# Where fourteen operand slots of a diffusion backbone lie in SBUF

## Chip, cores and metric

The kernel runs on one core of a Trainium2 chip. The metric is the device time of one execution in microseconds (us), smaller is better. "Offset" below is an SBUF address within a partition, in bytes, modulo 256.

## What is computed

A two-layer diffusion backbone over 512 latent tokens (LAT) with a prefix of 256 context tokens (CTX), width 1024, in float32:

```python
def swiglu(h, w_in, w_out):
    gate, up = jnp.split(h @ w_in, 2, axis=-1)
    return (jax.nn.silu(gate) * up) @ w_out
...
# layer i: half-step SwiGLU -> mixer (0 = short gated conv, 1 = GQA) -> half-step SwiGLU
h = norm_modulate(x_lat, norm_g[i, 0], m_lat[:, 0, 0], m_lat[:, 0, 1])
x_lat = x_lat + MACARON_WEIGHT * m_lat[:, 0, 2] * swiglu(h, ffn_w_in[i, 0], ffn_w_out[i, 0])
...
return rms_norm(x_lat, final_g)
```

Every sub-layer starts with an RMS norm, scaled and shifted by vectors that come from a conditioning vector, and ends in a gated residual. Layer 0 mixes by a gated convolution of width 3, layer 1 by attention with 8 query heads, 2 key heads and a two-dimensional rotary embedding. The FFN is 2816 wide.

## The kernel before

**Arithmetic.** A float32 product is made of three fp32r matmuls (mm3, lines 860 to 863): weights high x operand high (L861), weights high x operand low (L862), weights low x operand high (L863). "High" is the rounded value, "low" the remainder; ScalarE makes the high part and VectorE the low part (split, L189 and L190). Activations lie transposed, with features on the partitions and tokens along the free dimension, so the activation is the moving operand and a 128 x 128 block of weights the stationary one. Each matmul has its own weight load, which the profile lists as PEld.

**Seven products.** The first matmul of an FFN and of the convolution is done by a fast 2 x 2 scheme over halves of the features and of the tokens: seven products M1 to M7 take the place of eight. Each output chunk c takes one round. In a round TensorE runs M1 (operand B11), M2 (B21), M7 of the chunk before (T3), M5 (T1), M6 (T2), and of the chunk before M4 (T4) and M3 (B22). A product is 4 k-steps of 3 matmuls, 12 matmuls of 384 columns, or of 256 columns in the last FFN, where only the 512 latent tokens are left. The first two or three chunks of a sub-layer are done directly, with operands B11, B21, B12 and B22, while the sums T1 to T4 are still being made. The order is written out by hand (product_order) for TensorE and SyncE, and for stretches of VectorE and ScalarE.

**Slots.** The operands' high and low parts lie in fourteen slots of the pool xp, tags T0 to T13:

- in the rounds (T_SLOTS, line 68): B11 in 0 and 1, B21 in 2 and 3, B12 and later T4 in 4 and 5, T1 in 6 and 7, B22 in 8 and 9, T2 in 10 and 11, T3 in 12 and 13; in the last FFN (LAST_T_SLOTS, line 73) B12 and T4 in 6 and 7, T1 in 8 and 13, B22 in 9 and 10, T2 in 11 and 12, T3 in 4 and 5;
- when the rounds are over, slots 6 and 7, 10 and 11, 8 and 9 hold the last weights of the closing matmul (HELD_AFTER_T, line 71; "f00held", "c01held", "f02held" and "f10held" in the profile, three output blocks in each of the first two pairs, two in the third), and other pairs in the last FFN and the attention;
- between times they hold the normed tokens before the split, the first conditioning weights, the QKV operands (h in 0 to 3, hl in 4, 5, 8 and 9), the attention's probabilities p (0 to 3), its queries and its output.

The other matmul operands are the streamed weights w (pool wp), the gated activations gh and gl (tags G0 to G3), and vh and vl of the attention; all of them lie at offset 96 before and after.

**How a slot gets its place.** The pool x_all (24576 bytes, offset 96) comes first in xp. A tag of xp gets its place when the first tile with this tag is asked for, right behind the tag before, and it is as large as its largest tile. A tile of [4, 384] float32 has 6144 bytes = 24 x 256. Slots 4, 5, 8 and 9 also hold B12 and B22 of the very first FFN, which carry two more columns: [4, 386], 6176 bytes = 6144 + 32. So each of these four slots moves the offset of everything behind it by 32. The first use is by the conditioning weights (slots 6, 7, 8, then 9, 10, 11, then 4, 5, then 13), then by B11, B21 (0 to 3) and the normed tokens (12).

Of the kernel before, what the change touches and what calls it, by code (L numbers as in the profile page):

```python
# [10 lines left out]
F32 = mybir.dt.float32  # L11
# [7 lines left out]
P = 128  # L19
D = 1024  # L20
# [47 lines left out]
T_SLOTS = {"B11": (0, 1), "B21": (2, 3), "B12": (4, 5), "T4": (4, 5), "T1": (6, 7), "B22": (8, 9), "T2": (10, 11), "T3": (12, 13)}  # L68

F_SLOTS = {(0, 0): 12, (1, 0): 13, (0, 1): 10, (1, 1): 11}  # L70
HELD_AFTER_T = ((6, 7), (10, 11), (8, 9))

LAST_T_SLOTS = {"B11": (0, 1), "B21": (2, 3), "B12": (6, 7), "T4": (6, 7), "T1": (8, 13), "B22": (9, 10), "T2": (11, 12), "T3": (4, 5)}
# [56 lines left out]
def backbone(ctx: ExitStack, tc: tile.TileContext, a: dict, out: bass.AP):  # L130
# [4 lines left out]
    xp = ctx.enter_context(tc.tile_pool(name="xp", bufs=1))  # L135
# [202 lines left out]
    def add_products(key, sources, order, parts, direct, out_w, held, home=lambda c, kh: None, between=None):  # L338

        raw = {}  # L340
        seen = set()

        def need(c, which):
            if (c, which) not in raw:
                raw[c, which] = raw_add(sources[c][which], (1, KC), 2 if c < direct else 1)

        for c, which in ((0, 0), (0, 1), (1, 0), (1, 1)):
            need(c, which)
        for c, m in order:
            if m == "out":  # L350
                last = c == len(parts) - 1
                outs = out_w(c)
                add_out(*outs, held=held if last else None, key=f"{key}held", events=((key, "M5"), (key, "M6"), (key, "M3")))
                continue
            for which in range(2):
                need(c, which)
            if (c, m) == (0, "10") and between:
                between()
            if c >= direct:
                add_product(raw[c, 0], raw[c, 1], m)  # L360
            elif (c, m[1]) not in seen:
                seen.add((c, m[1]))
                k0 = 4 * int(m[1])
                for which in range(2):
                    where = home(c, int(m[1]))
                    add_plain(raw[c, which], 0, slice(k0, k0 + 4), where and ("home", (*where, which)))
# [46 lines left out]
    def w_list():  # L413
        def ffn_products(i, s, home=lambda c, kh: None, between=None):
            b = 2 * i + s // 2
            boot = (i, s) == (0, 0)
            held = {(1, 0): HELD_AFTER_T[:2], (1, 2): HELD_AFTER_LAST_T}.get((i, s), HELD_AFTER_T)
            sources = [[a["ffn_w_in"][b, f][:, z] for z in range(2)] for f in range(FC)]
            f0 = starts(FFN_PARTS)
            add_products(f"f{i}{s}", sources, ffn_order[boot], FFN_PARTS, BOOT_DIRECT if boot else FFN_DIRECT, lambda p: (a["ffn_w_out"][b], f0[p], FFN_PARTS[p]), held, home, between)  # L420
# [7 lines left out]
        sources = [[a["conv_w_in"][j][:, u] for j, u in pair] for pair in conv_pairs]  # L428
        add_products("c01", sources, conv_order, (6, 6), CONV_DIRECT, lambda p: (a["conv_w_out"], 4 * p, 4), HELD_AFTER_T)
        ffn_products(0, 2)  # L430
# [159 lines left out]


    x_all = xp.tile([P, KC, NT], F32, name="x", tag="x")
    stage = {}
    ssq = []
    hh, hl = [None] * KC, [None] * KC
# [125 lines left out]
    T, full = {}, {}  # L721
    geo = SimpleNamespace(tokens=TOKENS, half=NH, groups=BOTH, t_slots=T_SLOTS, f_slots=F_SLOTS)
    region = []
# [1171 lines left out]
```

## Time and profile before

| | |
|---|---|
| time, median of 3 runs | 2406.66 us (2406.36 to 2406.87) |
| span of the profiled execution | 2405.2 us |
| busy: TensorE, weight loads | 2383.8 us (99%), 2258.6 us (94%) |
| busy: VectorE, ScalarE, GpSimd | 2033.0 us (85%), 1164.8 us (48%), 135.2 us (6%) |
| granted TensorE clock | 0.999 |
| read from HBM | 249.16 MB, 104 GB/s over the span |

Busy time counts an instruction from its start to its end. Matmuls overlap: the next one starts before the one ahead of it has ended, so a matmul of 384 columns is listed with some 0.34 us while the next starts some 0.17 us later. What adds up to the span is the distance from start to start. The timeline shows starts to 0.01 us, so the pace of a group is read over many matmuls: the start of one product less the start of the product before is the time of 12.

### The profile page before, as it was taken

How to read it: one execution, taken by the hardware profiler on the slowest of the kernel's cores; microseconds unless marked ns; L12 is line 12 of the kernel's file. 1: busy time of each engine (PE TensorE's matmuls, PEld its weight loads, DVE VectorE, ACT ScalarE, POOL GpSimd, SP SyncE). 2: the span in 40 equal slices, each digit the busy share in tenths (PEclk: the TensorE clock that was granted, in tenths of full speed). 3: DMA queues.
4: the chain of work that ended last, by engine and by line, in shares of the span. 5: the costliest groups of instructions: out<-in, count | busy, mean ns of one | idle time of the engine just before them, and what ended most of it. 6: DMA issues, size and time to landing. Idle time of an engine off the chain costs nothing.

```text
span 2405.2 us, 37639 instructions
## 1 busy us (share of the span) xinstructions
PE 2383.8 (99%) x14303; PEld 2258.6 (94%) x14303; DVE 2033.0 (85%) x4018; ACT 1164.8 (48%) x2198; POOL 135.2 (6%) x256
## 2 busy tenths in 40 slices
PE   8999999999999999999999999999999999999998
PEld 6999999999999999999999999999998889999998
DVE  6989989978988888888887988888778987987787
ACT  5634334355535653433435543343355776555555
POOL 0001111100000001000000001101100000000000
PEclk9999999999999999999999999999999999999999
DMA  9234444430334123323432144443441101133331
GB/s 334 87 112 137 130 126 129 131 115 27 106 106 132 33 69 115 127 93 119 126 100 73 49 124 126 146 136 122 141 131 45 53 10 58 67 110 102 106 106 62
DMA packets 93062, 253.71 MB, mean 105 GB/s; under 512 B 10320, under 2 KB 18640, under 8 KB 92880
## 3 DMA queue, kind: packets, MB, share of 16 engines
q1 hardware_dynamic: 71984, 183.65, 23.5%
q0 software_dynamic: 20352, 67.12, 9.4%
q8 instruction: 112, 1.84, 0.3%
q14 instruction: 70, 0.57, 0.1%
q10 hardware_dynamic: 544, 0.52, 0.1%
HBM read 249.16 MB, written 2.10 MB: 104 GB/s over the span
## 4 chain that ended last, share of the span: by engine, by line
PE 92%; DVE 3%; ACT 2%; DMA 1%; issue 1%; SPq 0%; DVEq 0%; ACTq 0%
PE ps_A L861 16%; PE ps_A L862 16%; PE ps_A L863 16%; PE ps_C L862 11%; PE ps_C L861 11%; PE ps_C L863 11%; PE ps_B L863 3%; PE ps_B L861 3%; PE ps_B L862 3%; PE ps_T L1542 1%; DMA ada<-in_ada_w 1%; ACT pr L1525 0%; DMA raw<-in_ffn_w_in 0%; DVE w L190 0%; PE ps_O L861 0%
## 5 line engine op out<-in xcount | busy, mean ns | idle before, releaser
L189 ACT ACTIVATE w<-raw 128x512 fp32r<-128x512 f32 (+1 forms) x862 | 522.4, 619 | 721.0 <-PE ps_A L863 229.7
L190 DVE TENSOR_TENSOR w<-raw,w 128x512 fp32r<-128x512 f32 (+1 forms) x862 | 574.3, 679 | 119.7 <-ACT w L189 105.8
L509 POOL DMA_DIRECT2D aw<-in_ada_t x240 | 129.1, 538 | 1374.8 <-DVE mods L530 973.9
L373 DVE TENSOR_TENSOR raw<-raw,raw 128x512 f32<-128x512 f32 x264 | 181.5, 689 | 9.0 <-DMA raw<-in_ffn_w_in 4.9
L862 PE MATMUL ps_C<-gl,w 128*128 128x512 f32 (+1 forms) x548 | 188.5, 344 | 0.0
L861 PE MATMUL ps_C<-gh,w 128*128 128x512 f32 (+1 forms) x548 | 188.4, 344 | 0.0
L863 PE MATMUL ps_C<-gh,w 128*128 128x512 f32 (+1 forms) x548 | 188.2, 343 | 0.0
L861 PE MATMUL ps_A<-gh,w 128*128 128x512 f32 (+1 forms) x540 | 185.8, 344 | 0.6 <-DVE x L929 0.6
L862 PE MATMUL ps_A<-gl,w 128*128 128x512 f32 (+1 forms) x540 | 185.7, 344 | 0.0
L863 PE MATMUL ps_A<-gh,w 128*128 128x512 f32 (+1 forms) x540 | 185.5, 344 | 0.0
L530 DVE CUSTOM_DVE_ANT_0 ps_S<-aw,silu_row,packed 128x512 f32<-128x512 f32 x208 | 156.9, 754 | 2.4 <-DMA aw<-in_ada_t 1.0
L530 DVE CUSTOM_DVE_ANT_0 ps_S<-aw,silu_row,mods 128x512 f32<-128x512 f32 x208 | 156.8, 754 | 1.0
L929 DVE SCALAR_TENSOR_TENSOR x<-ps_C,gat,x 128x512 f32<-128x512 f32 (+1 forms) x158 | 99.5, 631 | 43.1 <-PE ps_C L863 42.7
L861 PE MATMUL ps_A<-tB11h,w 128*128 128x384 f32 (+1 forms) x400 | 130.8, 327 | 0.2 <-ACT tB11h L785 0.2
L862 PE MATMUL ps_A<-tB11l,w 128*128 128x384 f32 (+1 forms) x400 | 130.3, 326 | 0.2 <-DVE tB11l L786 0.2
L863 PE MATMUL ps_A<-tB11h,w 128*128 128x384 f32 (+1 forms) x400 | 130.4, 326 | 0.0
L862 PE MATMUL ps_C<-tB22l,w 128*128 128x384 f32 (+2 forms) x376 | 121.8, 324 | 0.0
L863 PE MATMUL ps_C<-tB22h,w 128*128 128x384 f32 (+2 forms) x376 | 121.7, 324 | 0.0
L861 PE MATMUL ps_C<-tB22h,w 128*128 128x384 f32 (+2 forms) x376 | 121.5, 323 | 0.0
L929 DVE SCALAR_TENSOR_TENSOR x<-ps_A,gat,x 128x512 f32<-128x512 f32 (+1 forms) x162 | 101.8, 637 | 17.0 <-PE ps_A L863 16.7
L863 PEld LDWEIGHTS ps_C<-gh,w 128*128 128x128 f32 x548 | 103.9, 190 | 12.3
L861 PEld LDWEIGHTS ps_A<-gh,w 128*128 128x128 f32 x540 | 102.4, 190 | 14.0 <-issue 1.0
(486 smaller groups left out, 6946.0 us busy)
## 6 DMA issues: line engine op xcount, KB each, us to landing
raw<-in_ffn_w_in SPq DMA_DIRECT2D x170, 512.0 KB, 3.7
aw<-in_ada_t POOLq DMA_DIRECT2D x240, 256.0 KB, 3.0
raw<-in_ffn_w_out SPq DMA_DIRECT2D x80, 512.0 KB, 4.1
raw<-in_conv_w_in SPq DMA_DIRECT2D x24, 512.0 KB, 3.7
ada<-in_ada_w SPq DMA_DIRECT2D x28, 256.0 KB, 5.7
raw<-in_attn_w_qkv SPq DMA_DIRECT2D x12, 512.0 KB, 4.9
raw<-in_ada_w SPq DMA_DIRECT2D x8, 512.0 KB, 6.8
silu_row<-in_crow POOLq DMA_DIRECT2D x8, 512.0 KB, 4.2
```

What stands on the lines that cost most here:

```text
L189: hi = act.activation(dsth, src, AF.Copy)
L190: lo = dve.tensor_tensor(out=dstl, in0=src, in1=dsth.bitcast(F32), op=ALU.subtract)
L373: dve.tensor_tensor(out=quad(o), in0=quad(x), in1=quad(y), op=ALU.subtract)
L509: nc.gpsimd.dma_start(w, a["ada_t"][t, kh, j])
L530: ins = dve.tensor_tensor_reduce(out=junk, in0=w, in1=silu_row[kh][:, v, :], scale=1.0, scalar=total if kh else ada_b[:, i, hm // 2, col : ...
L861: pe.matmul(ps, wh, xh, start=first, stop=False, **kw)
L862: pe.matmul(ps, wh, xl, start=False, stop=False, **kw)
L863: pe.matmul(ps, wl, xh, start=False, stop=last, **kw)
L929: dve.scalar_tensor_tensor(out=x, in0=p[:, o - off : o - off + w], scalar=gat[:, m, v : v + 1], in1=x, op0=ALU.mult, op1=ALU.add)
L1542: pe.transpose(pt[:, c, :], pr[:, (c0 + c) * P : (c0 + c + 1) * P], ident)
```

## The change

Two additions: a list of the slots, and a loop that asks for one tile of each tag in this order right after x_all, before anything else does. These tiles are never written or read. The shape is [3, 512] float32, 6144 bytes; the four tags with a larger tile later keep their 6176 bytes.

```diff
 F_SLOTS = {(0, 0): 12, (1, 0): 13, (0, 1): 10, (1, 1): 11}
+SLOT_ORDER = (6, 7, 10, 11, 12, 0, 1, 2, 3, 13, 8, 9, 4, 5)
 HELD_AFTER_T = ((6, 7), (10, 11), (8, 9))
...
     x_all = xp.tile([P, KC, NT], F32, name="x", tag="x")
+    for n in SLOT_ORDER:
+        xp.tile([P, 3, D // 2], F32, name=f"slot{n}", tag=f"T{n}")
```

Offsets of the slots in the built programs, in the order in which they lie:

| | 96 | 128 | 160 | 192 | 224 |
|---|---|---|---|---|---|
| before | 6, 7, 8 | 9 | 10, 11, 4 | 5 | 13, 0, 1, 2, 3, 12 |
| after | 6, 7, 10, 11, 12, 0, 1, 2, 3, 13, 8 | 9 | 4 | 5 | none |

The slots take the same stretch of SBUF as before, from byte 28768 to 114912, and nothing outside it moves. On each engine the two programs have the same instructions with the same operands, waits and signals in the same order; the addresses in them are all that differs.

## Prediction

> **What bounds the kernel now.** I read the page first, for the bound, then the waits of TensorE, then the costliest groups by form, and last the timeline, row by row, where one operand changes and nothing else does.
>
> ```profile
> span 2405.2 us, 37639 instructions
> ...
> PE 2383.8 (99%) x14303; PEld 2258.6 (94%) x14303; DVE 2033.0 (85%) x4018; ACT 1164.8 (48%) x2198; POOL 135.2 (6%) x256
> ...
> PE 92%; DVE 3%; ACT 2%; DMA 1%; issue 1%; SPq 0%; DVEq 0%; ACTq 0%
> ```
>
> ```profile
> PE ps_C L484 <- DMA ada<-in_ada_w: 4.6, 2, 4.2
> ```
>
> TensorE is busy 99% of the span and 92% of the chain that ended last; its longest wait in total is 4.6 us, at the start. So the time is the sum of the gaps between starts of matmuls, and what one gap gains the span gains. VectorE, at 85%, has room for a TensorE that goes a third of a per cent faster. The instructions keep their order and their waits, so all that the change can move is the length of single operations.
>
> A round of the seven products, 12 matmuls of 384 columns each, all with weights at offset 96 (modulo 256), looks so in the timeline (columns: start in us, duration):
>
> ```profile
> 901.09 0.34 PE L861 MATMUL ps_A<-tB11h,w 128*128 128x384 f32 x1
> ...
> 903.21 0.34 PE L861 MATMUL ps_B<-tB21h,w 128*128 128x384 f32 x1
> ...
> 905.32 0.34 PE L861 MATMUL ps_A<-tT3h,w 128*128 128x384 f32 x1
> ...
> 907.42 0.34 PE L861 MATMUL ps_C<-tT1h,w 128*128 128x384 f32 x1
> ...
> 909.51 0.33 PE L861 MATMUL ps_A<-tT2h,w 128*128 128x384 f32 x1
> ...
> 911.59 0.34 PE L861 MATMUL ps_A<-tT4h,w 128*128 128x384 f32 x1
> ...
> 913.69 0.34 PE L861 MATMUL ps_C<-tB22h,w 128*128 128x384 f32 x1
> ...
> 915.77 0.40 PE L861 MATMUL ps_C<-gh,w 128*128 128x512 f32 x1
> ```
>
> The same work takes 2.12, 2.11 and 2.10 us for B11, B21 and T3 (slots at 224), 2.09 for T1 (both at 96), 2.08 for T2 (160), 2.10 for T4 (160 and 192) and 2.08 for B22 (96 and 128). That is 6.33 us / 36 = 175.8 ns a matmul at 224 against 2.09 / 12 = 174.2 for T1.
>
> Is it the offset or the product? The closing pass of an FFN holds the moving operand still (g, at 96) and changes only the slots that hold the weights, in the order (6,7), (10,11), (8,9):
>
> ```profile
> 1275.56 0.34 PE L861 MATMUL ps_C<-gh,f02held 128*128 128x384 f32 x1
> ...
> 1281.81 0.34 PE L861 MATMUL ps_C<-gh,f02held 128*128 128x384 f32 x1
> ...
> 1288.16 0.33 PE L861 MATMUL ps_A<-gh,f02held 128*128 128x384 f32 x1
> ```
>
> 36 matmuls with weights in slots 6, 7 (at 96, like g) take 6.25 us, 173.6 ns each; the next 36, with weights in 10, 11 (at 160), take 6.35 us, 176.4 each. Slots 6 to 11 are neighbours in memory, the shapes are equal and no wait lies between. What counts, then, is how the offset of one operand stands to that of the other; equal offsets are among the best. With 512 and 256 columns (layer 1):
>
> ```profile
> 1787.77 0.40 PE L861 MATMUL ps_C<-gh,f10held 128*128 128x512 f32 x1
> ...
> 1795.94 0.40 PE L861 MATMUL ps_C<-gh,f10held 128*128 128x512 f32 x1
> ...
> 1804.34 0.39 PE L861 MATMUL ps_A<-gh,w 128*128 128x512 f32 x1
> ...
> 1809.81 0.28 PE L861 MATMUL ps_C<-gh,f10held 128*128 128x256 f32 x1
> ...
> 1814.12 0.39 PE L647 MATMUL ps_S<-th,ones_r 128*128 128x512 f32 x1
> ...
> 1814.58 0.28 PE L861 MATMUL ps_A<-gh,f10held 128*128 128x256 f32 x1
> ...
> 1818.82 0.28 PE L861 MATMUL ps_C<-gh,w 128*128 128x256 f32 x1
> ```
>
> At 512 columns equal offsets take 8.17 / 36 = 226.9 ns, weights at 160 take 8.40 / 36 = 233.3. At 256 columns the sign turns: 4.31 / 36 = 119.7 with equal offsets against 4.24 / 36 = 117.8 at 160. So the change gains on long matmuls and loses on short ones.
>
> **The change part by part.** It removes, adds and moves no instruction; the two new lines only fix places. Ten slots (6, 7, 10, 11, 12, 0, 1, 2, 3, 13) come to 96, the offset of w, g, vh and vl; slots 8, 9, 4 and 5 keep 96, 128, 160 and 192. So B22, T4 and B12 keep their price. The counts:
>
> ```profile
> L861 PE MATMUL ps_A<-tB11h,w 128*128 128x384 f32 x312 | 106.0, 340 | 0.2 <-ACT tB11h L785 0.2
> ...
> L861 PE MATMUL ps_B<-tB21h,w 128*128 128x384 f32 x272 | 92.1, 339 | 0.0
> ...
> L861 PE MATMUL ps_A<-tT3h,w 128*128 128x384 f32 x272 | 92.0, 338 | 0.0
> ...
> L861 PE MATMUL ps_C<-tT1h,w 128*128 128x384 f32 x272 | 91.2, 335 | 0.0
> ...
> L861 PE MATMUL ps_C<-tB11h,w 128*128 128x384 f32 x40 | 13.5, 338 | 0.0
> ...
> L861 PE MATMUL ps_A<-tB21h,w 128*128 128x384 f32 x32 | 11.1, 347 | 0.0
> ...
> L861 PE MATMUL ps_C<-tB21h,w 128*128 128x384 f32 x32 | 10.8, 338 | 0.0
> ```
>
> 1. *Slots 0 to 3, 12 and 13 from 224 to 96, 384 columns.* 312 + 272 + 272 + 40 + 32 + 32 = 960 triples of L861 to L863, 2880 matmuls. 175.8 becomes what equal offsets show: 174.2 at worst (T1, which follows a product at 224), 173.6 at best (36 in a row). After the change five products in a row are equal, so I take 173.6: 2880 x 2.2 ns = -6.3 us (ends -4.6 and -6.3). The mean durations say the same, 338 to 340 against 335; no other group differs in so many rows.
> 2. *T1, already at 96*, loses the neighbour at 224: 816 x 0.6 = -0.5 us (0 to -0.5).
> 3. *T2 from 160 to 96* (as many as T1): 2.08 / 12 = 173.3 becomes 173.6, +0.2 us (0 to +0.7, the upper end at 174.2).
> 4. *Weights held in slots 10, 11.* Three closing passes at 384 columns use them in two halves of 36: 216 x 2.8 = -0.6 us. In layer 1, 36 x 6.4 = -0.2 us. The pair (8,9) keeps its offsets. Nothing hides this, as TensorE does not wait there.
> 5. *QKV, 512 columns*: h lies in slots 0 to 3.
>
> ```profile
> L861 PE MATMUL ps_A<-gh,w 128*128 128x512 f32 x306 | 119.5, 391 | 0.6 <-DVE x L929 0.6
> ...
> L861 PE MATMUL ps_A<-h,w 128*128 128x512 f32 x64 | 25.2, 394 | 0.0
> ...
> L861 PE MATMUL ps_B<-h,w 128*128 128x512 f32 x16 | 6.3, 394 | 0.0
> ```
>
> h takes 3 ns more than g. 3 x (64 + 16) are 240 matmuls; hl stays where it is, so I take most of the difference, 2.5 ns: -0.6 us (0 to -1.0).
>
> 6. *The last FFN and the attention, 256 columns.* Three products of a round of the last FFN, and behind them the count of a product's k-steps there (20 rounds of 4) and of the attention's matmuls on p, from the groups by form:
>
> ```profile
> 2116.31 0.28 PE L861 MATMUL ps_A<-tT2h,w 128*128 128x256 f32 x1
> ...
> 2117.72 0.28 PE L861 MATMUL ps_A<-tT4h,w 128*128 128x256 f32 x1
> ...
> 2119.14 0.28 PE L861 MATMUL ps_C<-tB22h,w 128*128 128x256 f32 x1
> ```
>
> ```profile
> L861 PE MATMUL ps_O<-p,vh 128*128 128x256 f32 x96 | 28.3, 295 | 0.0
> ...
> L861 PE MATMUL ps_A<-tT2h,w 128*128 128x256 f32 x80 | 22.4, 281 | 0.0
> ```
>
> T2 (160 and 224 in that stage) takes 1.41 us for 12, 117.5 ns each, T4 (both at 96) 1.42, 118.3. After the change B11, B21, T1 and T2 join T4: 5 x 240 matmuls at most at the 119.7 of the held weights, at least at T4's own 118.3. From some 118 that is 1200 x 1.7 = +2.0 at the top, +0.3 at the bottom. The 3 x 96 matmuls on p (slots 0 to 3, now equal to vh and vl) give 0 to 288 x 1.7 = +0.5 by the same step, and the few weights held in these stages I put at 0 to +0.2, an estimate from the same 1.7. The two ends are equally near, so I take the middle, +1.4 us (+0.3 to +2.7; middle 1.5, less a little as T4 is the nearer row).
>
> 7. *Other engines on the moved slots.*
>
> ```profile
> L802 DVE TENSOR_TENSOR tB11l<-f,tB11h 128x768 fp32r<-128x768 f32 x8 | 7.6, 951 | 1.0 <-ACT tB11h L800 1.0
> ...
> L190 DVE TENSOR_TENSOR tT1l<-f,tT1h 128x768 fp32r<-128x768 f32 x8 | 7.3, 954 | 0.1
> ```
>
> VectorE takes 951 ns at 224 and 954 at 96: nothing. What is late next is nothing either: a round that is 0.1 us shorter needs the same splits, which fill 85% of the span.
>
> Sum: -6.3 - 0.5 + 0.2 - 0.6 - 0.2 - 0.6 + 1.4 = -6.6 us on the span of 2405.2. The median, 2406.66 us, lies 1.5 us above the span, and that part stays: 2406.66 - 6.6 = 2400.1 us, 0.27% faster. The ends together: at best -6.3 - 0.5 - 0.8 - 1.0 + 0.3 = -8.3, at worst -4.6 + 0.7 - 0.8 + 2.7 = -2.0, so 2398.4 to 2404.7; all bad ends at once are unlikely.
>
> [...]
>
> **The rivals.** *No effect* (0.09): the 224 slots form one stretch of memory, and B11, B21 and T3 are always on it, so offset and product cannot be told apart in the seven products alone; it might be the bank or the order of the products. Against it stand the held weights. Time 2406.7, give or take 0.3. [...]
>
> *Slower* (0.05): the offset of both operands being equal is good only for g, whose chunks lie in another area, and bad for slots packed at one offset. Then the 2880 matmuls stay at 175.8, T1 and T2 rise to that (816 x 1.6 + 816 x 2.5 = 3.3 us), and the 256-column stages take their worst, +2.7: 2412.7. It decides if equal offsets cost more than 175.8. T1 at 174.2, both slots at 96, speaks against it.
>
> **How the numbers follow.** Forecast 0.86, no effect 0.09, slower 0.05. Within the forecast, 2397.8 to 2404.3 holds some nine in ten (the upper ends of the 256 columns and T1's pace for all); times 0.86 that is 0.8, so the range stops there and leaves the rivals out. 0.2% is 4.8 us, about what a measurement of this kernel can tell from no change. The forecast passes it unless 1.8 us of its 6.6 are missing: 0.72 faster; 0.25 within (0.14 of the forecast, the no-effect rival, some of the slower one); 0.03 slower.
>
> **What would show it.** In the profile after, B11, B21 and T3 should start 2.08 us apart with mean durations of 335, the pair (10,11) should take 6.25 us for 36, h 391 at 512 columns, and the last FFN's T2 1.42 to 1.44. I am wrong if B11 stays at 2.12 (the offset is not the cause), if TensorE shows new waits, or if the short matmuls give back more than 2.7 us.

## The result, and the profile after

The changed kernel takes 2401.7 us (median of 13 runs, 2401.17 to 2402.41) against 2406.7 us before (13 runs, 2406.36 to 2407.33): a ratio of 0.9979, with a 95% interval of 0.9972 to 0.9986. Forecast were 2400.1 us, with a range of 2397.8 to 2404.3. The granted clock was 0.999 as before.

The page after, first, gives the bound:

```profile
span 2399.9 us, 37639 instructions
...
PE 2379.0 (99%) x14303; PEld 2253.2 (94%) x14303; DVE 2032.3 (85%) x4018; ACT 1166.2 (49%) x2198; POOL 135.4 (6%) x256
...
PE 92%; DVE 3%; ACT 3%; DMA 1%; issue 1%; SPq 0%; DVEq 0%; ACTq 0%
```

Its longest wait on TensorE in total:

```profile
PE ps_C L485 <- DMA ada<-in_ada_w: 4.6, 1, 4.6
```

The instructions are as many as before, TensorE is as busy in share, and its longest wait is the same 4.6 us. The span went from 2405.2 to 2399.9 us with nothing but the gaps between matmuls to give it. So the timeline is to be read row by row. The round that the prediction showed looks so after the change (start in us, duration; the lines of mm3 are L864 to L866 now):

```profile
897.31 0.34 PE L864 MATMUL ps_A<-tB11h,w 128*128 128x384 f32 x1
...
899.39 0.33 PE L864 MATMUL ps_B<-tB21h,w 128*128 128x384 f32 x1
...
901.48 0.33 PE L864 MATMUL ps_A<-tT3h,w 128*128 128x384 f32 x1
...
903.55 0.33 PE L864 MATMUL ps_C<-tT1h,w 128*128 128x384 f32 x1
...
905.63 0.33 PE L864 MATMUL ps_A<-tT2h,w 128*128 128x384 f32 x1
...
907.72 0.33 PE L864 MATMUL ps_A<-tT4h,w 128*128 128x384 f32 x1
...
909.81 0.34 PE L864 MATMUL ps_C<-tB22h,w 128*128 128x384 f32 x1
...
911.89 0.40 PE L864 MATMUL ps_C<-gh,w 128*128 128x512 f32 x1
...
1270.18 0.34 PE L864 MATMUL ps_C<-gh,f02held 128*128 128x384 f32 x1
...
1276.43 0.33 PE L864 MATMUL ps_C<-gh,f02held 128*128 128x384 f32 x1
...
1282.67 0.33 PE L864 MATMUL ps_A<-gh,f02held 128*128 128x384 f32 x1
```

B11, B21 and T3 start 2.07 to 2.09 us apart, where it was 2.10 to 2.12; the whole round takes 14.58 us, where it was 14.68. Of the weights that are held in slots, the first two pairs now take the same 6.25 and 6.24 us; the second one had taken 6.35.

The groups by form give the mean durations (the number ahead of the second bar) over all rounds:

```profile
L864 PE MATMUL ps_A<-tB11h,w 128*128 128x384 f32 x312 | 105.1, 337 | 0.2 <-ACT tB11h L788 0.2
...
L864 PE MATMUL ps_B<-tB21h,w 128*128 128x384 f32 x272 | 90.9, 334 | 0.0
...
L864 PE MATMUL ps_A<-h,w 128*128 128x512 f32 x64 | 25.2, 394 | 0.0
```

B11 went from 340 to 337 ns, B21 from 339 to 334; h of the QKV stage stayed at 394. To see where in the program the time went, the starts of two stages, QKV and last FFN, are enough, first before:

```profile
1821.70 0.39 PE L861 MATMUL ps_A<-h,w 128*128 128x512 f32 x1
...
2046.64 0.28 PE L861 MATMUL ps_A<-tB11h,w 128*128 128x256 f32 x1
```

And after, with three products of a round of the last FFN behind them:

```profile
1813.89 0.40 PE L864 MATMUL ps_A<-h,w 128*128 128x512 f32 x1
...
2039.09 0.28 PE L864 MATMUL ps_A<-tB11h,w 128*128 128x256 f32 x1
...
2099.14 0.28 PE L864 MATMUL ps_A<-tT2h,w 128*128 128x256 f32 x1
...
2100.58 0.28 PE L864 MATMUL ps_A<-tT4h,w 128*128 128x256 f32 x1
...
2102.02 0.28 PE L864 MATMUL ps_C<-tB22h,w 128*128 128x256 f32 x1
```

| stage | before, us | after, us | difference |
|---|---|---|---|
| start to QKV (384 and 512 columns) | 1821.70 | 1813.89 | -7.8 |
| QKV and attention | 224.94 | 225.20 | +0.3 |
| last FFN to the end (256 columns) | 358.6 | 360.8 | +2.2 |

(The last row is the span less the start.) Everything up to QKV gains, and the stage with short matmuls loses: T2 takes 1.44 us for 12 matmuls where it took 1.41, and so does T4 (it took 1.42), though its own offsets are what they were. The table at the end gives the pace by the distance of the two offsets.

### The profile page after: what moved, and what is told of

It reads as the page before. It is cut to its first block, busy times and chain, and to the rows that moved or that the text cites. A ratio compares the mean times of both kernels' runs of the same rounds, so it can differ in the third digit from the quotient of the medians.

```text
span 2399.9 us, 37639 instructions
## 1 busy us (share of the span) xinstructions
PE 2379.0 (99%) x14303; PEld 2253.2 (94%) x14303; DVE 2032.3 (85%) x4018; ACT 1166.2 (49%) x2198; POOL 135.4 (6%) x256
## 4 chain that ended last, share of the span: by engine, by line
PE 92%; DVE 3%; ACT 3%; DMA 1%; issue 1%; SPq 0%; DVEq 0%; ACTq 0%
PE ps_A L864 16%; PE ps_A L865 16%; PE ps_A L866 16%; PE ps_C L865 11%; PE ps_C L866 11%; PE ps_C L864 11%; PE ps_B L866 3%; PE ps_B L864 3%; PE ps_B L865 3%; PE ps_T L1545 1%; DMA ada<-in_ada_w 0%; DVE f L766 0%; DMA raw<-in_ffn_w_in 0%; ACT pr L1528 0%; PE ps_O L866 0%
## 5 line engine op out<-in xcount | busy, mean ns | idle before, releaser
L864 PE MATMUL ps_C<-gh,w 128*128 128x512 f32 (+1 forms) x548 | 188.2, 343 | 0.0
L866 PE MATMUL ps_C<-gh,w 128*128 128x512 f32 (+1 forms) x548 | 188.0, 343 | 0.0
L864 PE MATMUL ps_A<-gh,w 128*128 128x512 f32 (+1 forms) x540 | 185.5, 343 | 0.6 <-DVE x L932 0.6
L866 PE MATMUL ps_A<-gh,w 128*128 128x512 f32 (+1 forms) x540 | 185.3, 343 | 0.0
L864 PE MATMUL ps_A<-tB11h,w 128*128 128x384 f32 (+1 forms) x400 | 129.9, 325 | 0.2 <-ACT tB11h L788 0.2
L866 PE MATMUL ps_A<-tB11h,w 128*128 128x384 f32 (+1 forms) x400 | 129.3, 323 | 0.0
L866 PE MATMUL ps_C<-tB22h,w 128*128 128x384 f32 (+2 forms) x376 | 121.5, 323 | 0.0
L864 PE MATMUL ps_C<-tB22h,w 128*128 128x384 f32 (+2 forms) x376 | 121.2, 322 | 0.0
L864 PEld LDWEIGHTS ps_A<-gh,w 128*128 128x128 f32 x540 | 102.3, 189 | 14.0 <-issue 1.0
L866 PEld LDWEIGHTS ps_C<-gh,w 128*128 128x128 f32 x548 | 103.8, 189 | 12.3
```

Of the source, the lines that this page charges most:

```text
L864: pe.matmul(ps, wh, xh, start=first, stop=False, **kw)
L866: pe.matmul(ps, wl, xh, start=False, stop=last, **kw)
```

## The experiments

The theory: the pace of a matmul is set by how the offset of its moving operand stands to that of its weights, modulo 256. The rivals: it is the place in SBUF or the neighbour in memory; or it is uniformity, that is, that all slots have one offset, whichever it is. All kernels have the instructions, waits and order of the changed kernel, and only addresses differ. Where the loop over the slots gets pads, it has this form, and only the two tables above it change:

```diff
+PADS = {13: 128, "end": 128}
     for n in SLOT_ORDER:
+        if n in PADS:
+            xp.tile([P, PADS[n] // 4], F32, name=f"pad{n}", tag=f"pad{n}")
         xp.tile([P, 3, D // 2], F32, name=f"slot{n}", tag=f"T{n}")
+    xp.tile([P, PADS["end"] // 4], F32, name="pade", tag="pade")
```

Paces below are medians over all runs of 12 matmuls of one operand in a trace, start to start, in ns.

**pad_only: the order of before, with a pad.** The slots stay in the order in which they lay before the change; 128 bytes ahead of slot 13 bring the six slots from 224 to 96. Slots 10 and 11 stay at 160.

```diff
-SLOT_ORDER = (6, 7, 10, 11, 12, 0, 1, 2, 3, 13, 8, 9, 4, 5)
+SLOT_ORDER = (6, 7, 8, 9, 10, 11, 4, 5, 13, 0, 1, 2, 3, 12)
+PADS = {13: 128, "end": 128}
```

> Slots in the order of before, each where it lay, but 128 bytes of padding ahead of slot 13 and 128 behind the last slot: 13, 0, 1, 2, 3 and 12 move from offset 224 to 96 by 128 bytes, all else keeps its place and offset. Theory (the offset of the moving operand against that of the weights sets the pace): B11, B21 and T3 start 2.08 us apart in place of 2.10 to 2.12, T1 2.08; T2 (160) keeps 2.08, weights held in 10 and 11 keep 6.35 us for 36; in the last FFN B11 and B21 rise to 1.43 or 1.44. Time about 2406.7 - 6.9 + 1.0 = 2400.8 us. Rival (the place in SBUF or the product makes it, the move of 20 to 40 KB was what helped): B11, B21, T3 stay at 2.10 to 2.12, time 2406.7. Rival (the ten slots must equal each other): not met here either, 2406.7.

Measured: 2402.1 us (2401.68 to 2402.35, 11 runs), ratio 0.9981 (0.9972 to 0.9990). Its timeline shows the same round and the same held weights:

```profile
899.74 0.33 PE L868 MATMUL ps_B<-tB21h,w 128*128 128x384 f32 x1
...
901.82 0.33 PE L868 MATMUL ps_A<-tT3h,w 128*128 128x384 f32 x1
...
903.90 0.33 PE L868 MATMUL ps_C<-tT1h,w 128*128 128x384 f32 x1
...
1276.78 0.34 PE L868 MATMUL ps_C<-gh,f02held 128*128 128x384 f32 x1
...
1283.13 0.33 PE L868 MATMUL ps_A<-gh,f02held 128*128 128x384 f32 x1
```

B21 and T3 take 2.08 us as after the change, and the weights in 10 and 11, which keep 160, the old 6.35 (1276.78 to 1283.13). The gain comes with the offset and without the new order: the rival of the place falls. The time is 1.3 us above the expected 2400.8; a part of that is the last FFN, which takes 360.2 us, 1.6 more than before, where 1.0 had been allowed for.

**all_224: the order of after, everything 128 bytes further.** All ten slots and slot 8 have one offset, but it is 224, 128 away from the weights; the other three are at 0, 32 and 64.

```diff
+PADS = {6: 128, "end": 128}
```

> The order of after with 128 bytes of padding ahead of slot 6 and 128 behind the last slot: the ten slots and slot 8 equal each other at 224, the weights stay at 96. Theory (offset against the weights): all of B11, B21, T3, T1 and T2 take 2.11 us as slots at 224 did before, the pair (6,7) as held weights is no longer equal to g; time about 2406.7 + 68 x (24 + 35 ns) = 2410.7, with B22, T4 and B12 at new offsets (224/0, 32/64) 2407 to 2415. Rival (what counts is that the ten slots equal each other): 2401.7 as after, B11 2.08.

Measured: 2413.86 us (2413.44 to 2414.28, 5 runs), ratio 1.0030 (1.0018 to 1.0043). The round:

```profile
909.69 0.34 PE L868 MATMUL ps_C<-tT1h,w 128*128 128x384 f32 x1
...
911.81 0.34 PE L868 MATMUL ps_A<-tT2h,w 128*128 128x384 f32 x1
...
913.92 0.34 PE L868 MATMUL ps_A<-tT4h,w 128*128 128x384 f32 x1
```

T1 and T2, the two that were fast before, now take 2.12 and 2.11 us like the others. Uniformity alone makes the kernel slower than before (2413.9 us against 2406.7); that rival falls too.

**w_160 and w_plus_256: the weights move instead.** The slots stay as after the change; the streamed weights w go 64 bytes further, to offset 160, and a second pad of 192 bytes keeps what lies behind them at its offset. In the control everything from w on goes 256 bytes further, and all offsets stay.

```diff
+    wp.tile([P, 16], F32, name="padw", tag="padw", bufs=1)
+    ctx.enter_context(tc.tile_pool(name="wpad", bufs=1)).tile([P, 48], F32, name="padv", tag="padv")
```

> The layout of after, but the streamed weights w moved by 64 bytes to offset 160 (and the pools behind them kept where they were). Theory: every product on a slot at 96 takes what held weights at 160 took, 2.12 us at 384 columns, and g 2.80 us for 12 at 512 columns, 1.41 at 256: (82 + 83 + 3 x 68) x 38 ns = +14.0, 145 x 80 ns = +11.6, 109 x -27 ns = -2.9, last FFN about -2: 2401.7 + 21 = 2422 (2417 to 2428, B22, T4 and B12 at differences not seen before). Rival (the offset of the slots alone counts): 2401.7.

```diff
+    wp.tile([P, 64], F32, name="padw", tag="padw", bufs=1)
```

> A control: the layout of after with w and everything behind it moved by 256 bytes, so that every address of w changes and no offset modulo 256 does. Theory: nothing changes, 2401.7, products 2.08 us, g 2.72 and 1.44. Rival (the modulus is larger than 256, say 512): the slots at 96 stand 256 from w in one of the two layouts and not in the other, and 384 columns go to 2.09 or more and the time by some us.

Measured: the control 2401.8 us (2401.14 to 2402.57, 10 runs), the same as after the change; w_160 2411.64 us (2411.27 to 2412.69, 8 runs), ratio 1.0022 (1.0012 to 1.0032). One product of a round (B11) and 12 matmuls of the closing pass in w_160's timeline:

```profile
901.56 0.34 PE L866 MATMUL ps_A<-tB11h,w 128*128 128x384 f32 x1
...
903.66 0.34 PE L866 MATMUL ps_B<-tB21h,w 128*128 128x384 f32 x1
...
1008.56 0.40 PE L866 MATMUL ps_C<-gh,w 128*128 128x512 f32 x1
...
1011.36 0.40 PE L866 MATMUL ps_A<-gh,w 128*128 128x512 f32 x1
```

No slot moved, and yet the products take 2.10 us instead of 2.08, and 12 matmuls of 512 columns 2.80 instead of 2.72. 64 bytes more in the weights' address cost 9.9 us, 256 bytes nothing. So the offset of the weights counts as well as that of the moving operand; that it is the difference of the two shows in w_32 below. The direction was as expected and the size was half: the expectation took 2120 ns for 384 columns, from the held weights at 160, and the streamed weights at 160 gave 2095. Why the two differ was not found. The pace changes with either address while the other stays: T1 takes 2080 ns after and 2095 in w_160, where only the weights move; B21 takes 2109 ns before and 2080 after, where only the slots move.

**g_160, g_128, g_64: only the gated activations move.** They are the moving operand of the closing matmuls, and go 64 and 32 bytes up and 32 bytes down. The names tell the offset; the weights stay at 96. The diff is that of g_160, and the same two lines stand once more in the pools of the last FFN; g_128 has 8 and 56 in the place of 16 and 48, g_64 has 56 and 8.

```diff
+        gp.tile([P, 16], F32, name="padg", tag="padg")
+        qp.tile([P, 48], F32, name="padq", tag="padq")
```

> The layout of after, but the gated activations g (tags G0 to G3, all FFN and convolution outputs) moved by 64 bytes to offset 160, weights at 96 as ever. Theory, from T2 at 160 in before: 256 columns fall from 1.44 to 1.41 us for 12, 109 x -27 ns = -2.9 us and the closing passes with held weights at 96 at 384 columns stay at 2.08; at 512 columns no row shows a moving operand 64 above the weights: 2.72 for 12 if like 384 columns (then 2398.8), up to 2.80 as with weights 64 above the operand (then 2410). Rival (offsets matter only for slots in xp): 2401.7.

> The layout of after with g moved by 32 bytes to offset 128, 32 above the weights, a difference that no pure row has shown. If the pace goes smoothly with the difference: 512 columns between 2.72 (equal) and 2.75 us (64 above), 256 columns between 1.44 and 1.41: 2400 to 2402.5. If it depends on a step of 64 or 128 bytes, 32 above is like equal: 2401.7.

> The layout of after with g moved to offset 64, 32 below the weights. If the pace goes smoothly with the difference: 512 columns between 2.72 (equal) and 2.80 us (64 below, as weights at 160 with g at 96), 256 columns between 1.44 and 1.41, closing passes at 384 columns between 2.08 and 2.12: 2402 to 2409. If only the size of the difference counts, as g_128.

Measured: g_160 2401.28 us (2400.38 to 2401.57, 9 runs), g_128 2408.68 us (2408.12 to 2409.18, 8 runs), g_64 2410.75 us (2410.32 to 2411.71, 8 runs). In g_160, 12 matmuls on g of 256 columns:

```profile
931.85 0.28 PE L864 MATMUL ps_A<-gh,w 128*128 128x256 f32 x1
...
933.21 0.28 PE L864 MATMUL ps_A<-gh,w 128*128 128x256 f32 x1
```

In g_128 and in g_64, 12 of 512 columns:

```profile
1096.79 0.39 PE L864 MATMUL ps_C<-gh,w 128*128 128x512 f32 x1
...
1099.59 0.40 PE L864 MATMUL ps_A<-gh,w 128*128 128x512 f32 x1
```

```profile
1099.36 0.39 PE L864 MATMUL ps_C<-gh,w 128*128 128x512 f32 x1
...
1102.16 0.40 PE L864 MATMUL ps_A<-gh,w 128*128 128x512 f32 x1
```

64 above the weights, 256 columns take 1.36 us here, as in 46 of the 115 runs of 12 on g; nearly all others take 1.41 (1440 ns with equal offsets). 512 columns take 2747 ns as the median, against 2720; the two nearly cancel. I had expected the steps of 32 to lie between, and they don't: at 32 above as at 32 below, 512 columns take 2800, and both kernels come out above what was expected of a smooth price. The price is not smooth in the distance, and the two sides are not alike at 64: w_160 has the slots and g 64 below the weights, and there 512 columns take 2800 as well.

Nor does the distance fix the pace alone. In g_128, weights held in slots 6 and 7 meet the same part of g in the second half of two closing passes, that of the first FFN (f00held) and that of the convolution (c01held). Slots, addresses and shapes are the same, and each pair of lines is 36 matmuls apart:

```profile
532.70 0.34 PE L864 MATMUL ps_A<-gh,f00held 128*128 128x384 f32 x1
...
538.94 0.34 PE L864 MATMUL ps_A<-gh,f00held 128*128 128x384 f32 x1
...
782.25 0.34 PE L864 MATMUL ps_A<-gh,c01held 128*128 128x384 f32 x1
...
788.61 0.34 PE L864 MATMUL ps_A<-gh,c01held 128*128 128x384 f32 x1
```

That is 6.24 us against 6.36. Just ahead of both stand 12 matmuls on the same slots, at 2120 ns, and two of a norm's sums at the same offsets; VectorE and ScalarE are equally busy beside them (5.5 and 3.8 of 7 us). Of the 36 runs of 12 with both slots at 96 (6, 7, 10 and 11) in that kernel, 22 take 2080 ns and 14 take 2120. The same is seen in g_160: 512 columns on streamed weights take 2746 to 2762 ns in 117 of 151 runs and some 2800 in 33, 256 columns 1360 or 1413, and a stretch of 36 matmuls mostly keeps one value to its end. So some distances have two paces, and what decides between them stays open: it is not the offsets of the group or of what ran just ahead.

**equal_13: all slots but 9 at the offset of the weights.** Three more slots (4, 5, 8) come to 96, so that T4, B12 and most of hl are equal too.

```diff
-SLOT_ORDER = (6, 7, 10, 11, 12, 0, 1, 2, 3, 13, 8, 9, 4, 5)
+SLOT_ORDER = (6, 7, 10, 11, 12, 0, 1, 2, 3, 13, 4, 5, 8, 9)
+PADS = {5: 224, 8: 224, "end": 64}
```

> Thirteen slots at 96: the order of after with 4, 5, 8, 9 at the end and padding of 224 bytes ahead of 5 and of 8, so that 4, 5 and 8 equal the rest, 9 is at 128. Theory: T4 and B12 (4, 5) fall from 2.10 to 2.08 us, -1.2 and -0.3 us; T3 of the last FFN (4, 5) rises from 1.42 to 1.44, +0.4 us; and h in QKV, which kept its pace in after although h was at 96, falls from 232 to 227 ns a matmul at 512 columns because hl, read between, now equals it in six of eight k-steps: -1.3 us. Together 2399.3. Rival for QKV (offsets don't set the pace there, the other engines' traffic or the shape of h does): h stays at 231 to 233 ns, 2400.6.

Measured: 2402.07 us (median of 10 runs; one of them, at 3619.49 us, is an outlier), ratio 0.9981 (0.9972 to 0.9991): no better than the changed kernel. T4 and B22 in its round, and from the groups by form that of h:

```profile
906.92 0.33 PE L868 MATMUL ps_A<-tT4h,w 128*128 128x384 f32 x1
...
909.00 0.33 PE L868 MATMUL ps_C<-tB22h,w 128*128 128x384 f32 x1
...
911.10 0.40 PE L868 MATMUL ps_C<-gh,w 128*128 128x512 f32 x1
```

```profile
L868 PE MATMUL ps_A<-h,w 128*128 128x512 f32 x64 | 25.0, 391 | 0.0
```

T4 gains what was expected (2098 to 2080 ns), and the mean duration of h comes down to 391 ns. But B22 behind it, whose slots are at 96 and 128 in both kernels, rises from 2080 to 2101 ns: +1.4 us over the 82 products seen. What changed for B22 is T4 ahead of it (and its place in memory, by multiples of 256). So the pace of a product depends also on the product ahead of it; T1 in the next run, whose slots do not move at all, shows the same (2080 to 2105 ns). The expectation priced each operand by itself and so missed this.

**mix: offsets by the length of the matmul.** Before the change T2, at 160 against weights at 96, had been the fastest product at both lengths (2075 ns at 384 columns; 1403 at 256, where its low part lay at 224). So slots 13, 0 to 3, 12, 4 and 5 go to 160; 6, 7, 10, 11 and 8 stay at 96, as held weights are slow at 160, and 9 at 128.

```diff
-SLOT_ORDER = (6, 7, 10, 11, 12, 0, 1, 2, 3, 13, 8, 9, 4, 5)
+SLOT_ORDER = (6, 7, 10, 11, 8, 9, 13, 0, 1, 2, 3, 12, 4, 5)
+PADS = {5: 224, "end": 32}
```

> Slots 6, 7, 10, 11, 8 at 96 and 9 at 128 (they hold weights in the closing passes and stay equal to g), slots 13, 0, 1, 2, 3, 12, 4, 5 at 160, 64 above the weights. Theory: at 384 columns a pair 64 above the weights takes 2.08 us as T2 in before, so B11, B21, T3 and now T4 take 2.08 (T4 -1.2 us); at 256 columns a pair at 160 takes 1.41 to 1.42, so B11, B21 and T3 of the last FFN fall from 1.44, 1.44 and 1.42 (-1.3 us) and T1, T2 and T4 there lose the neighbours that held them at 1.44 (-0.8 us). Time 2401.7 - 3.3 = 2398.4 (2397.5 to 2400.5). Rival (equal offsets are what 384 columns need): B11, B21, T3 go to 2.10 and more, 2401 to 2408.

Measured: 2398.76 us (2398.53 to 2399.48, 6 runs), ratio 0.9968 (0.9955 to 0.9980). The last FFN takes 358.5 us, as before the change, and the 384-column stages keep their gain. T3, at 160, keeps 2080 ns, and it is T1 behind it, equal to w at 96, that takes more, 2.10 us:

```profile
901.84 0.34 PE L868 MATMUL ps_A<-tT3h,w 128*128 128x384 f32 x1
...
903.92 0.34 PE L868 MATMUL ps_C<-tT1h,w 128*128 128x384 f32 x1
...
906.02 0.33 PE L868 MATMUL ps_A<-tT2h,w 128*128 128x384 f32 x1
```

**w_32: nearly every moving operand 64 above the streamed weights.** The distance +64 cost nothing at 384 columns (T3 2080 ns in mix, as with equal offsets) and gained at 256 (g 1413 ns in g_160 against 1440). So w goes to 32, and g and all slots but 9 lie at 96, where g and held weights are equal.

```diff
+PADS = {4: 192, 5: 224, "end": 32}
...
+    ctx.enter_context(tc.tile_pool(name="wpad", bufs=1)).tile([P, 16], F32, name="padv", tag="padv")
```

> Twelve operand slots and slot 8 of after, now with 4 and 5 too, and g stay at 96 (9 at 128); the streamed weights w alone move to offset 32, so that every one of these operands stands 64 above w, and weights held in the slots still equal g. Theory, from the rows of 64 above: 384 columns 2.08 us for 12 in B11, B21, T3, T1, T2 and T4; 256 columns 1.40 to 1.42 us in the last FFN and 1.40 in g; 512 columns 2.75 in g; held weights 2.08 and 2.72. Against mix: T1 -1.7 us, the last FFN's T1, T2, T4 -1.4, g about -0.5, h -0.5, B22 (64 and 96 above) 0 to +0.8: 2398.8 - 3.7 = 2395.1 (2393.5 to 2397.5). Rival (what helped mix was slots at two different offsets, which break up a lock at 256 columns): with nearly all at one difference the last FFN goes back to 1.44, 2400 or more.

Measured: 2397.33 us (2397.31 to 2397.75, 5 runs), ratio 0.9961 (0.9947 to 0.9975). It is the fastest of all: 9.4 us below the kernel before, 4.4 below the changed one, with no run in the range of that one's. Its B22, and three products of the last FFN:

```profile
909.19 0.34 PE L869 MATMUL ps_C<-tB22h,w 128*128 128x384 f32 x1
...
911.29 0.40 PE L869 MATMUL ps_C<-gh,w 128*128 128x512 f32 x1
...
2104.74 0.28 PE L869 MATMUL ps_C<-tT1h,w 128*128 128x256 f32 x1
...
2106.15 0.28 PE L869 MATMUL ps_A<-tT2h,w 128*128 128x256 f32 x1
...
2107.56 0.28 PE L869 MATMUL ps_A<-tT4h,w 128*128 128x256 f32 x1
```

The other products of 384 columns take 2080 ns as after the change, those of 256 columns 1.41 us instead of 1.44, and B22 pays, 2.10 us: +1.7 us over the rounds against the changed kernel, and +0.8 against mix, the upper end of what had been expected. Against mix 3.7 us were expected and 1.4 came: h kept its time (-0.5 expected), and B11, B21 and T3 of the last FFN, some of which ran at 1360 ns in mix, take 0.5 us more.

g stands 64 above w here as in g_160, but at 96 over 32 instead of 160 over 96, and the medians are the same, 2747 and 1413 ns. So for g, at these two places, it is the difference of the two offsets that counts, and not where either lies.

## Why the prediction was right, and where not

**The mechanism** held at each point that was tested: the offset without the order (pad_only), the order without the offset (all_224), and the weights moved instead of the slots (w_160), with 256 bytes as the control. The rival of no effect fell with the result and with the first of these. The slower rival needed equal offsets at 175.8 ns a matmul; they take 173.3. What it feared exists, but at another distance: in all_224 the packed slots lie 128 from the weights, and that kernel is slower than before (2413.9 us against 2406.7).

**Terms 1 to 4, the 384-column stages and the held weights: right in size.** Forecast were -6.3 - 0.5 + 0.2 - 0.6 - 0.2 = -7.4 us. Over the products found in the traces, mean pace less mean pace times their number gives B21 -2.5, B11 -2.0, T3 -2.0, which is -6.5 for term 1; T1 -0.4, T2 +0.35, the held weights -0.7 and -0.24. T4, forecast at nothing, gave -0.3. Together that is -7.8, and the stages up to QKV became 7.8 us shorter. The choice of 173.6 ns for a matmul among equal neighbours, the lower end, was borne out: 2080 / 12 = 173.3.

**Term 5, QKV: wrong.** The step said that h takes 3 ns more than g, that "hl stays where it is, so I take most of the difference", -0.6 us. h stayed at 394 ns, and 12 matmuls at 2781 (2777 before): +0.1 us over them. What slows h there is not its own offset. When equal_13 moved most of hl to 96, h went to 391 ns and 2750, and the h products took 0.5 us less in all. So h's pace goes with the hl matmul that stands between two on h, which the forecast took for a bystander. That is not the whole, as g with all offsets equal takes 2720.

**Term 6, 256 columns: right in sign, too small.** The forecast was +1.4 us, the middle between 118.3 ns (T4 of before, both slots equal to w) and 119.7. The last FFN became 2.2 us longer, the attention some 0.2: +2.4, still below the upper end of 2.7. The step that failed is that T4 was "the nearer row". T4 stood among products at other offsets. With equal neighbours T4, T2 and B21 all take 1440 ns, 120.0 a matmul; T2 alone gave +0.7 us, B11, T4, B21 and T1 about +0.3 each. The held weights, a closed series, had been the better row, as in term 1. The forecast allowed for neighbours with T1 and forgot them here. It also had B22 keep its price, but in the last FFN B22's low part lies in slot 10, which moves from 160 to 96: 1426 ns became 1431 as the mean of 12, +0.1 us.

**Term 7: right.** VectorE's busy time is 2032.3 us (2033.0 before), and no new wait came up on TensorE.

In sum -7.8 + 0.1 + 2.4 = -5.3 us, which is what the span shows (2405.2 to 2399.9), against -6.6 forecast; the medians differ by 5.0.

What stays open: why the weights held in slots at 160 took 2120 ns at 384 columns and the streamed ones at 160 took 2095; what decides between the two paces that some distances have (in g_160, with weights 64 below g, 512 columns take 2800 on the held weights and in 33 of 151 runs on streamed ones, some 2750 in nearly all the rest); and what in the chip makes the offset count. Only the dependence is shown, not its cause.

## What to carry to other kernels

In this kernel TensorE is busy 99% of the span, its longest wait comes to 4.6 us, and addresses alone moved the time between 2397.3 us (w_32) and 2413.9 us (all_224). Where a trace looks like that, the addresses of the operands are worth a try: read the distance from start to start over a dozen matmuls, per operand, and compare it with the offset modulo 256 of the moving tile and of the weights. Price a group by a row whose neighbours already look as they will after the change, since here the pace of one product also went with the one ahead (B22, 2080 to 2101 ns in equal_13), and by more than one stretch, since one distance had two paces (2080 and 2120 ns in g_128). And the best offset was not the same at each length (12 matmuls on g with equal offsets and 64 above: 2720 and 2747 ns at 512 columns, 1440 and 1413 at 256), so that a layout is settled by the sum over all stages, and by a run.

## What the runs showed of the hardware

The pace of one fp32r matmul with a weight load of its own, in ns, by the moving operand's offset less the weights', from medians of 12 (two values where the runs fall into two groups):

| distance, bytes | 384 columns | 512 columns | 256 columns |
|---|---|---|---|
| 0 (after; slots, and g at 512) | 173.3 | 226.7 | 120.0 |
| +64 (w_32; g_160) | 173.3 | 228.9, 233.3 | 113.3, 117.7 |
| 128 (before, B11, B21, T3; all_224) | 175.8 to 176.4 | 232.6 | 118 to 120 |
| +32 (g_128) | 173.3, 176.7 | 233.3 | 116.7 |
| -32 (g_64) | 173.3 | 233.3 | 118.6 |
| -64 (w_160; before, held 10 and 11) | 174.6; 176.7 | 233.3 | 117.7 |

The spread is 2% at 384 columns, 3% at 512 and 6% at 256, and no distance is best at all three lengths. The 512 columns at 128 are g against weights held at 224 in all_224; the 384 columns of g_128 and g_64 are g against weights held at 96, the rest of their rows streamed weights. It was not expected that 32 bytes of distance at 512 columns cost more than 64 upward (2800 ns for 12 against 2747), nor that a product whose own offsets don't change moves by 1% with the product ahead of it (B22, 2080 to 2101 ns in equal_13; T1, 2080 to 2105 in mix; T4 in the last FFN from before to after, 1421 to 1440). Nor was it expected that one distance has two paces (g_128, 384 columns: 2080 and 2120 ns with the same addresses).
